# A two-group encoder layer: the opening in a fixed order with the filter network first, and output sums kept in SBUF with products of 512 columns

## The chip, the cores and the metric

The kernel runs on one core of one Trainium2 chip. The metric is the device time of one execution in microseconds (us). All data comes from DRAM and goes back to it within that time. The engines of a core are named as in the profile: PE (TensorE, matrix products), PEld (its weight loads), DVE (VectorE), ACT (ScalarE), POOL (GpSimd) and SP (SyncE, which here issues every DMA).

## What is computed

One encoder layer is applied to two groups of tokens with the same weights: P, the prompt, of 1024 tokens, and S, the sample, of 512. Each token has D = 1024 channels. Everything is fp32.

```
h = rmsnorm(x, norm_g);  z = h @ w_in            # 4096 columns
hy_in, hy_gate, att_qkv, att_gate = split(z)     # 1536, 512, 1536, 512
x0, x1, vv = split(short_conv(hy_in))
f1 = sin(fr1 * (z_pos @ f_w1 + f_b1))            # the filter network, on positions only
f2 = sin(fr2 * (f1 @ f_w2 + f_b2))
kfilt = (f2 @ f_w3) * decay
y_hy  = rmsnorm(x0 * fft_conv(x1 * vv, kfilt), on_hy) * silu(hy_gate)
y_att = rmsnorm(neighbourhood_attention(q, k, v, rpb), on_att) * silu(att_gate)
out = x + concat(y_hy, y_att) @ w_out
```

The attention has 8 heads of 64 channels; tokens stand on a grid 64 wide, and each looks at a window of 8 rows and 16 columns.

## The kernel before, in words

**Numbers.** Every fp32 product is made of three products of rounded halves: a value is split into `hi` (the value rounded to fp32r, a cast) and `lo` (the rest, a subtraction), and hi·hi, lo·hi and hi·lo are summed in PSUM. So a weight unit of 128x512 takes a cast `whi` (L364) and a subtraction `wlo` on POOL (L365).

**Order.** A scheduler of the tile framework puts each engine's instructions into an order, by priorities and a timeline of its own; `high_priority(n)` in the code raises them. Phases are generators that `weave` steps in turn, by fractions that `plan` takes from a list in `run` (L1129). Weight units are loaded and split ahead of use in the order of that plan (`fetch_w`, `issue_w`, `take_w`). All DMAs are issued on SP, one queue, in the order there.

**The opening (0 to 75 us).** `x_norm` (L217) loads four tiles of x (128 tokens x 1024) for each half of P, squares them on ACT with a sum along the row (L229), and DVE makes 1/sqrt of the mean from the sums by shift and three Newton steps (`rsqrt`, L203), then scales the four tiles. `x_turn` (L236) transposes them on PE (L247); ACT writes `hThi` (L249) and DVE `hTlo`. The filter network (`filters_mlp`, L155) runs beside it in segments of 512 positions: a product (L164), then on DVE the argument of the sine reduced to one period (`arg`, `n`), then Sin on ACT (L178). Its last results are `hm_p` and `hm_s`. `w3`, `fc` and `dftm` are constants that are split in the same stretch.

**265 to 885 us** hold the Hyena branch of P, then P's attention beside the Hyena branch and projections of S. The change alters nothing there but `rsqrt`.

**The projections (75 to 265 us)** make q, k, v of P (`proj_tok`, L404, `proj_ch`, L391) beside the spectra of the filters, whose decay tables `dec` come from DRAM.

**The output phase (from 885 us).** Attention of S runs beside the product with w_out, which has two parts: part 0 multiplies the Hyena rows of w_out (y_hy), part 1 the attention rows (y_att). There are three jobs of 512 tokens: P0, P1 and S. A job first loads its four operands `A` (128 channels x 512 tokens), and splits each into `hi` and `lo` (L1073 and a POOL subtraction). Part 0 of P0 and P1 comes first, then their part 1, then part 0 of S, and when the attention is over part 1 of S. For each 256 columns of w_out (two weight units) and each pair of token tiles, 24 products of 128x256 go into one PSUM bank (L1094). P0 and S gather their sums in `acc` in SBUF, which is first loaded with x. P1 does not: ACT copies its part 0 to `oo` (L1106), a DMA stores it to `sum` in DRAM, and in part 1 it is read back as `oy`, x as `ox`, both are added on POOL, and DVE adds the product.

The attention of S ends with `ya`, a 128x512 output block for each pair of heads: DVE multiplies it by the gate `ga_s` (loaded into a tile `qkr`), a DMA stores it as `A_s`, and the output phase loads it again as `lo`.

## Time and profile before

| what | value |
| --- | --- |
| device time, median of 3 runs | 1091.8 us (1089.95 to 1094.8) |
| the profiled execution | 1090.92 us, span of the profile 1089.1 us |
| granted clock of PE, mean | 0.982 |
| busy in the span | PE 92%, PEld 83%, DVE 73%, ACT 43%, POOL 38% |
| chain that ended last | PE 48%, DVE 27%, DMA 12% |

The span is the execution as the profiler saw it on the core. Busy shares are averages over phases with different limits, so what one phase is worth is read in that phase. A row of a timeline gives the start, the duration and, in brackets, how long the engine was idle before and what released it. The granted clock is a share of full speed: 1.00 is 2.4 GHz, 0.50 is 1.2 GHz.

### The profile page before, as it was taken

What the parts mean: (1) busy time and instruction counts of PE and PEld (TensorE: products, weight loads), DVE (VectorE), ACT (ScalarE), POOL (GpSimd) and SP (SyncE); (2) the same over time, 40 slices, a digit from 0 to 9 for tenths busy, and PEclk for the clock granted to TensorE, in tenths of its full rate; (3) what the DMA queues carried; (4) which work ended last, traced back from release to release, by engine and by line L of the source; (5) the groups of instructions that cost most, each with busy time, mean ns of one, the idle gap of its engine ahead of it and who ended that gap; (6) DMA issues with size and microseconds to landing.
All of it is one profiled execution on the core that took longest, in us unless ns stands there. A gap on an engine that the chain in (4) does not pass through costs nothing.

```text
span 1089.1 us, 18072 instructions
## 1 busy us (share of the span) xinstructions
PE 1003.6 (92%) x6444; PEld 906.6 (83%) x6444; DVE 800.1 (73%) x2134; ACT 463.1 (43%) x958; POOL 415.5 (38%) x336
## 2 busy tenths in 40 slices
PE   3898999988999999999989999987989989899997
PEld 2698999977788888888877887876968879899987
DVE  5997779552157767967559999887967977587874
ACT  6453334233331323122124565655747653476530
POOL 2032332112142323123256344354254356784651
PEclk9999999999999999999989999999999999999999
DMA  8226372756312121212483354435544478966522
GB/s 299 69 78 195 119 235 91 242 161 241 109 39 80 58 62 58 67 54 92 173 240 106 94 145 130 129 100 168 141 133 115 132 237 263 295 183 211 173 72 97
DMA packets 112216, 154.84 MB, mean 142 GB/s; under 512 B 7953, under 2 KB 80475, under 8 KB 111615
## 3 DMA queue, kind: packets, MB, share of 16 engines
q1 hardware_dynamic: 112127, 153.69, 45.3%
q8 instruction: 51, 0.84, 0.3%
q14 instruction: 38, 0.31, 0.1%
HBM read 110.35 MB, written 43.32 MB: 141 GB/s over the span
## 4 chain that ended last, share of the span: by engine, by line
PE 48%; DVE 27%; DMA 12%; issue 5%; ACT 4%; SPq 2%; POOL 1%; POOLq 0%; DVEq 0%; ACTq 0%
PE bank L391 25%; PE bank L1094 7%; PE bank L443 3%; PE bank L404 3%; DMA dec<-in_dec_p_dram 2%; PE bank L1012 2%; SPq L60 2%; DVE zc L63 2%; DMA v_p<-vg 2%; DMA v_s<-vg 2%; PE bank L445 2%; PE bank L444 2%; DVE s_sb L981 2%; PE bank L1003 2%; DVE s L63 1%
## 5 line engine op out<-in xcount | busy, mean ns | idle before, releaser
L365 POOL TENSOR_TENSOR wlo<-wraw,whi 128x512 fp32r<-128x512 f32 x160 | 233.7, 1464 | 514.3 <-ACT whi L364 322.5
L391 PE MATMUL bank<-hThi_p,whi 128*128 128x512 f32 x320 | 126.8, 396 | 3.9 <-DVE vg L63 3.2
L391 PE MATMUL bank<-hThi_p,wlo 128*128 128x512 f32 x320 | 126.7, 396 | 0.0
L391 PE MATMUL bank<-hTlo_p,whi 128*128 128x512 f32 x320 | 126.3, 395 | 0.0
L404 PE MATMUL bank<-whi,hThi_p 128*128 128x256 f32 x384 | 111.6, 293 | 6.3 <-DVE vg L63 3.2
L1094 PE MATMUL bank<-whi,hi 128*128 128x256 f32 x384 | 111.6, 292 | 6.0 <-ACT oo L1106 2.6
L1094 PE MATMUL bank<-whi,lo 128*128 128x256 f32 x384 | 110.7, 292 | 0.9 <-POOL lo L63 0.9
L1094 PE MATMUL bank<-wlo,hi 128*128 128x256 f32 x384 | 110.9, 290 | 0.0
L404 PE MATMUL bank<-wlo,hThi_p 128*128 128x256 f32 x384 | 110.6, 289 | 0.0
L404 PE MATMUL bank<-whi,hTlo_p 128*128 128x256 f32 x384 | 108.4, 287 | 0.0
L985 ACT ACTIVATE s_sb<-s_sb,mx 128x360 f32<-128x360 f32 (+1 forms) x96 | 60.3, 629 | 88.2 <-DVE mx L981 87.8
L364 ACT CAST whi<-wraw 128x512 fp32r<-128x512 f32 x66 | 40.9, 623 | 108.0 <-PE bank L391 72.9
L1094 PEld LDWEIGHTS bank<-whi,hi 128*128 128x128 f32 x384 | 75.4, 196 | 7.4 <-ACT oo L1106 2.8
L404 PEld LDWEIGHTS bank<-whi,hThi_p 128*128 128x128 f32 x384 | 74.2, 194 | 8.2 <-DVE vg L63 3.7
L364 DVE CAST whi<-wraw 128x512 fp32r<-128x512 f32 x94 | 58.6, 626 | 27.6 <-POOL lo L63 6.8
L1094 PEld LDWEIGHTS bank<-whi,lo 128*128 128x128 f32 x384 | 74.6, 196 | 1.6 <-POOL lo L63 1.6
L404 PEld LDWEIGHTS bank<-wlo,hThi_p 128*128 128x128 f32 x384 | 74.5, 194 | 1.0 <-issue 1.0
L1094 PEld LDWEIGHTS bank<-wlo,hi 128*128 128x128 f32 x384 | 75.2, 196 | 0.0
L391 PEld LDWEIGHTS bank<-hThi_p,whi 128*128 128x128 f32 x320 | 60.4, 189 | 17.1 <-DVE vg L63 4.1
L404 PEld LDWEIGHTS bank<-whi,hTlo_p 128*128 128x128 f32 x384 | 73.3, 193 | 0.3 <-issue 0.2
L391 PE MATMUL bank<-hThi_s,whi 128*128 128x512 f32 x160 | 65.6, 413 | 8.4 <-DVE vg L63 4.9
L1012 PE MATMUL bank<-pt,V 120*64 120x256 f32 (+1 forms) x352 | 66.5, 295 | 6.6 <-DVE pt L63 4.2
(279 smaller groups left out, 2765.8 us busy)
## 6 DMA issues: line engine op xcount, KB each, us to landing
wraw<-in_w_ch_dram SPq DMA_DIRECT2D x40, 512.0 KB
wraw<-in_w_tk_dram SPq DMA_DIRECT2D x24, 512.0 KB
wraw<-in_w_out_dram SPq DMA_DIRECT2D x16, 512.0 KB
V<-v_p SPq DMA_DIRECT2D x32, 240.0 KB
v_p<-vg SPq DMA_DIRECT2D x32, 160.0 KB
K_p<-Kw SPq DMA_DIRECT2D x4, 1088.0 KB
x<-in_x_prompt_dram SPq DMA_DIRECT2D x8, 512.0 KB
dec<-in_dec_p_dram SPq DMA_DIRECT2D x16, 256.0 KB
```

What stands on the lines that cost most here:

```text
L60: eng.dma_start(out=out, in_=in_)
L63: (eng or self.nc.vector).tensor_tensor(out=out, in0=a, in1=b, op=op)
L364: next(self.w_round)(out=hi, in_=r)
L365: nc.gpsimd.tensor_tensor(out=lo, in0=r, in1=f32(hi), op=ALU.subtract)
L391: nc.tensor.matmul(ps, lhsT=w, rhs=h[s][:, k], start=(k == 0 and i == 0), stop=(k == KC - 1 and i == 2))
L404: nc.tensor.matmul(pss[t // 2][:, t % 2, :], lhsT=h[t // 4][:, k, t % 4 * P:(t % 4 + 1) * P], rhs=w, start=(k == 0 and i == 0 and t % 2 == ...
L443: mm(o, lhsT=c, rhs=z, start=True, stop=False)
L444: mm(o[:, 0:P], lhsT=ns if inverse else s, rhs=z[:, 1], start=False, stop=False)
L445: mm(o[:, P:], lhsT=s if inverse else ns, rhs=z[:, 0], start=False, stop=True)
L985: nc.scalar.activation(out=s_sb[:, :n], in_=s_sb[:, :n], func=AF.Exp, bias=mx, scale=-1.0, accum_out=l)
L1012: nc.tensor.matmul(o, lhsT=vl, rhs=pr_, start=(c == 0 and i == 0), stop=(c == ncu - 1 and i == 1))
L1094: nc.tensor.matmul(ps[:, j, :], lhsT=h[:, tok], rhs=w, start=(k == 0 and i == 0 and j == 0), stop=(k == 3 and i == 2 and j == 1))
```

## The change

It has four parts.

1. In the opening z_p and the filter network's first two weights are loaded ahead of x, and the network's first segment stands ahead of the norm. DVE's order there is the order of the code (`manual_schedule`): first segment, norm and turn of half 0, norm and turn of half 1, and only then the other segments.
2. The sine's argument takes two multiply-adds instead of three, a Newton step of `rsqrt` three instructions instead of four.
3. The first two `wlo` are made by DVE, the others by POOL as before.
4. In the output phase products have 512 columns, every job has its `acc` in SBUF (no `sum`, `oo`, `oy`, `ox`), the Hyena rows of all three jobs are multiplied in one pass over the weights, and eight halves of weights may stand ready from the start. The attention rows of S remain for the end.

```
 rsqrt, in the loop of three:
-            self.mul(t, t, h)
-            self.ts(t, t, -0.5, ALU.mult, 1.5, ALU.add)
-            self.mul(y, y, t)
+            self.stt(t, t, -0.5, h, ALU.mult)
+            self.stt(y, t, 1.5, y, ALU.mult, ALU.add)
 sine argument:
-                self.stt(arg, n, -c1, arg)
-                self.stt(arg, n, -c2, arg)
-                self.stt(arg, n, -c3, arg)
+        self.stt(arg, n, -c1, arg)
+        self.stt(arg, n, c1 - TWO_PI, arg)
 setup, issue_w:
+        self.w_low = itertools.chain([nc.vector] * 2, itertools.repeat(nc.gpsimd))
-            nc.gpsimd.tensor_tensor(out=lo, in0=r, in1=f32(hi), op=ALU.subtract)
+            self.sub(lo, r, f32(hi), next(self.w_low))
 run, the opening:
-        with self.tc.high_priority(4000):
-            self.x_norm(Gp, xp, [lambda: None] * 3 + [self.issue_w] + [lambda: None] * 3 + [self.issue_w])
-            self.x_turn(Gp, (hp0, hp1))
-        self.mlp_load()
-        for _ in zip(self.filters_mlp(Gp, mp), self.filters_mlp(Gs, mp)):
-            pass
+        with self.tc.high_priority(4000), self.tc.manual_schedule(engines={self.nc.vector.engine}):
+            self.mlp_load(Gp)
+            self.mlp_seg(Gp, mp, 0, 0)
+            self.x_norm(Gp, 0, xp)
+            self.issue_w()
+            self.x_turn(Gp, 0, hp0)
+            self.x_norm(Gp, 1, xp)
+            self.issue_w()
+            self.x_turn(Gp, 1, hp1)
+            self.mlp_load(Gs)
+            self.mlp_seg(Gp, mp, 0, 1)
+            self.mlp_seg(Gs, mp, 0, 0)
+        for G, sg in ((Gp, 0), (Gp, 1), (Gs, 0)):
+            self.mlp_seg(G, mp, 1, sg)
 run, the plan and the output phase:
-            [(["out0", "out1", "out0"], (0.0, 0.97), 0), (["att_s"], (0.0, 0.9), 4000)],
-            [(["out1"], every, 0)],
+            [(["out0", "out1"], (0.0, 0.97), 0), (["att_s"], (0.0, 0.9), 4000)],
+            [(["out1s"], every, 0)],
-                dict(G=Gp, seg=1, ops=pools["ops1"], first=pools["first"], last=pools["last"]),
+                dict(G=Gp, seg=1, ops=pools["ops1"], accs=pools["acc1"]),
+        self.w_pools, self.w_bufs = itertools.cycle((wp, self.wp)), 8
-        self.weave(self.chain(self.out_part(0, jobs[:2]), self.then(more_w), self.out_part(1, jobs[:2]), self.out_part(0, jobs[2:])),
-                   self.attention(Gs, ap))
+        self.weave(self.chain(self.out_part(0, jobs), self.out_part(1, jobs[:2])), self.attention(Gs, ap))
 load_w (new), for w_out; other weights are loaded as before:
+        _, h, part, u = key
+        for g in range(2):
+            self.dma(raw.rearrange("p (k g c) -> p k g c", k=2, g=2)[:, :, g],
+                     self.io["w_out"][h * 2 + g, part].rearrange("p (k c) -> p k c", k=4)[:, u * 2:u * 2 + 2])
 out_part, behind the loads of the operands, as it is now:
+        for h in range(2):
+            hs = slice(h * 512, (h + 1) * 512)
+            units = [self.take_w(("w_out", h, part, k // 2)) for k in range(4)]
             for jb in jobs:
+                G, t0, acc = jb["G"], jb["seg"] * 4, jb["acc"]
                 r = G.ratt if part else G.rhy
+                if part == 0:
+                    self.dma(acc[:, :, hs], G.x[t0 * P:(t0 + 4) * P, hs].rearrange("(t p) c -> p t c", p=P))
+                for t in range(4):
+                    ps = self.bank(next(self.mm_tags))
+                    tok = slice(t * P, (t + 1) * P)
+                    for k, (whi, wlo) in enumerate(units):
+                        hi, lo = jb["hi"][k][:, tok], jb["lo"][k][:, tok]
+                        for i, (w, a) in enumerate(((whi, hi), (wlo, hi), (whi, lo))):
+                            nc.tensor.matmul(ps, lhsT=a, rhs=w, start=(k == 0 and i == 0), stop=(k == 3 and i == 2))
+                    o = acc[:, t, hs]
+                    self.stt(o, ps, r[:, t0 + t:t0 + t + 1], o)
                     if part == 1:
+                        self.dma(G.out[(t0 + t) * P:(t0 + t + 1) * P, hs], o)
+                yield
```

`mlp_seg` is one segment of `filters_mlp`, `x_norm` and `x_turn` are now called once for each half.

What moves is the order on the engines. First DVE in the opening, from the first scaling of x on. Before (`rs_...` are steps of the second half's `rsqrt`, `w3lof`, `w3lob`, `fc` and `dftm` splits of constants, `arg` and `n` the filter network):

```order
L79 TENSOR_SCALAR x<-x,rs_y_201 128x1024 x4
L75 SCALAR_TENSOR_TENSOR hTlo_p<-bank,pc,hThi_p 128x512 x3
L81 TENSOR_SCALAR rs_h_249<-ss 128x4
L79 TENSOR_SCALAR rs_y_250<-rs_h_249 128x4
L81 TENSOR_SCALAR rs_y_250<-rs_y_250 128x4
L63 TENSOR_TENSOR w3lof<-w_477,w3f 64x512 x2
L63 TENSOR_TENSOR rs_t_251<-rs_y_250 128x4
L81 TENSOR_SCALAR arg<-bank,pc 128x512
L63 TENSOR_TENSOR fc<-fc 128x512
L63 TENSOR_TENSOR w3lob<-w_477,w3b 64x512 x2
```

There the second scaling follows after 39 more rows, with network steps all between them. The same stretch now:

```order
L80 TENSOR_SCALAR x<-x,rs_y_207 128x1024 x4
L64 TENSOR_TENSOR wlo<-wraw,whi 128x512 x2
L76 SCALAR_TENSOR_TENSOR hTlo_p<-bank,pc,hThi_p 128x512 x3
L64 TENSOR_TENSOR fc<-fc 128x512
L64 TENSOR_TENSOR w3lof<-w_467,w3f 64x512 x2
L64 TENSOR_TENSOR dftm<-km_481 128x256
L64 TENSOR_TENSOR dftm<-km_485 128x256
L64 TENSOR_TENSOR w3lob<-w_467,w3b 64x512 x2
L76 SCALAR_TENSOR_TENSOR hTlo_p<-bank,pc,hThi_p 128x512 x3
```

No `arg` or `n` stands there any more; five more `dftm`, two more `hTlo` and the second `rsqrt` lead to the second scaling, behind which eight `hTlo` stand together ahead of the next `arg`:

```order
L64 TENSOR_TENSOR rs_t_312<-rs_y_311 128x4
L76 SCALAR_TENSOR_TENSOR rs_t_312<-rs_t_312,rs_h_310 128x4
L76 SCALAR_TENSOR_TENSOR rs_y_311<-rs_t_312,rs_y_311 128x4
L80 TENSOR_SCALAR x<-x,rs_y_311 128x1024 x4
L76 SCALAR_TENSOR_TENSOR hTlo_p<-bank,pc,hThi_p 128x512 x8
L82 TENSOR_SCALAR arg<-bank,pc 128x512
```

The second place is SP at the end of the program. Before, the last four reloads of A_s (`lo_...`) stood together, behind the attention's last loads:

```order
L60 DMA qkr<-in_rpb_dram 128x1x488
L60 DMA A_s_108<-ya 128x512
L60 DMA V<-v_s_124 120x3x128
L60 DMA V<-v_s_125 120x3x128
L60 DMA lo_12096<-A_s_106 128x512
L60 DMA lo_12097<-A_s_107 128x512
L60 DMA lo_12098<-A_s_108 128x512
L60 DMA qkr<-ga_s_113 128x512
L60 DMA A_s_109<-ya 128x512
L60 DMA lo_12099<-A_s_109 128x512
L60 DMA out_dram<-acc 128x2x256 x8
```

Now each stands near the store that it reads, with loads of the attention behind it (the numbers of the tiles are others, `A_s_107` and `A_s_108` are the last two blocks):

```order
L61 DMA qkr<-in_rpb_dram 128x1x488
L61 DMA A_s_107<-ya 128x512
L61 DMA out_dram<-acc 128x512
L61 DMA lo_11432<-A_s_107 128x512
L61 DMA out_dram<-acc 128x512
L61 DMA V<-v_s_123 120x3x128
L61 DMA out_dram<-acc 128x512
L61 DMA V<-v_s_124 120x3x128
L61 DMA qkr<-ga_s_112 128x512
L61 DMA A_s_108<-ya 128x512
L61 DMA lo_11433<-A_s_108 128x512
L61 DMA out_dram<-acc 128x512 x8
```

The gate `ga_s` of the last block no longer has three reloads ahead of it. On PE the output products stand, by count, before the first transposes of the sample's attention (L929) 187 before and 84 now, from there to its last value product (L1012) 758 and 423, behind that 207 and 69; one of the products now is as wide as two before.

## Rows read from the trace of the kernel before

**Rows 1.** The page, busy time and share of the span of each engine.

```profile
PE 1003.6 (92%) x6444; PEld 906.6 (83%) x6444; DVE 800.1 (73%) x2134; ACT 463.1 (43%) x958; POOL 415.5 (38%) x336
```

**Rows 2.** Windows by phase: length, busy PE, PEld, DVE, ACT, POOL, clock, DMA share, GB/s.

```profile
0.00:75.00 75.00, 51.67 (x365) 45.64 (x366) 61.59 (x135) 44.00 (x77) 11.85 (x16) 0.98 0.43 155
75.00:265.00 190.00, 177.00 (x1313) 168.52 (x1311) 126.78 (x394) 66.01 (x164) 49.61 (x38) 0.99 0.53 176
...
885.00:1089.00 204.00, 186.76 (x1478) 183.02 (x1478) 145.15 (x353) 88.64 (x199) 121.63 (x110) 0.97 0.63 196
```

**Rows 3.** Timeline of DVE: start, us, line, operation, out<-in, shapes, count, idle before.

```profile
10.08 0.17 DVE L81 TENSOR_SCALAR rs_h<-ss 128x4 f32<-128x4 f32 x1 [10.08 <-ACT xsq L229]
...
10.89 1.22 DVE L63 TENSOR_TENSOR rs_t<-rs_t,rs_h 128x4 f32<-128x4 f32 x1
...
17.20 2.74 DVE L79 TENSOR_SCALAR x<-x,rs_y 128x1024 f32<-128x1024 f32 x4
21.24 2.07 DVE L75 SCALAR_TENSOR_TENSOR hTlo_p<-bank,pc,hThi_p 128x512 fp32r<-128x512 f32 x3 [1.29 <-ACT hThi_p L249]
...
23.93 1.38 DVE L63 TENSOR_TENSOR w3lof<-w,w3f 64x512 fp32r<-64x512 f32 x2
...
44.19 2.74 DVE L79 TENSOR_SCALAR x<-x,rs_y 128x1024 f32<-128x1024 f32 x4
...
73.89 0.69 DVE L63 TENSOR_TENSOR hm_s<-arg,hm_s 64x512 fp32r<-64x512 f32 x1
...
1060.07 1.75 DVE L75 SCALAR_TENSOR_TENSOR ya<-ya,pc,qkr 128x512 f32<-128x512 f32 x1 [1.18 <-DMA qkr<-ga_s]
```

**Rows 4.** Timeline of PE, opening and output phase.

```profile
42.67 2.07 PE L164 MATMUL bank<-h_p,w 128*128 128x512 f32 x2 [4.21 <-DVE arg L81]
...
939.06 0.39 PE L1094 MATMUL bank<-whi,hi 128*128 128x256 f32 x1 [2.63 <-ACT oo L1106]
...
1054.18 0.75 PE L1012 MATMUL bank<-pt,V 120*64 120x256 f32 x5
...
1070.52 0.28 PE L1094 MATMUL bank<-wlo,hi 128*128 128x256 f32 x1
...
1084.67 0.28 PE L1094 MATMUL bank<-whi,lo 128*128 128x256 f32 x1
```

**Rows 5.** The chain that ended last: start, us, what.

```profile
87.64 7.25 DMA dec<-in_dec_p_dram
...
280.71 33.17 PE bank L391 x145
...
925.99 12.07 DMA sum<-oo
...
1061.85 1.99 DMA A_s<-ya
1063.90 2.59 DMA lo<-A_s
...
1068.60 1.68 PE bank L1094 x12
```

**Rows 6.** Timeline of SP's queue, opening and end: start, us of issue, what.

```profile
1.19 1.84 SPq L60 DMA_DIRECT2D x<-in_x_prompt_dram  x4
...
7.55 1.63 SPq L60 DMA_DIRECT2D w<-in_w_dram  x2
10.11 0.31 SPq L60 DMA_DIRECT2D z_p<-in_z_p_dram  x1
...
1054.02 2.34 SPq L60 DMA_DIRECT2D lo<-A_s  x3
```

**Rows 7.** Timeline of ACT, the table load and the first two Sin.

```profile
39.85 1.28 ACT L178 ACT_TABLE_LOAD   x1
41.15 1.15 ACT L178 ACTIVATE h_p<-arg 128x512 f32<-128x512 f32 x2
```

**Rows 8.** Timeline of POOL in the opening.

```profile
10.82 4.94 POOL L365 TENSOR_TENSOR wlo<-wraw,whi 128x512 fp32r<-128x512 f32 x4 [9.51 <-ACT whi L364]
```

More of the change, by code (lines that the diff above doesn't have):

```diff
@@ L156, in filters_mlp, with mlp_seg @@
+    def mlp_seg(self, G, mp, layer, s):
         nc = self.nc
[L157 to L182 removed]
@@ new lines, in mlp_seg @@
+        w, b, fr = self.w12[layer], self.v[f"b{layer + 1}"], self.v[f"fr{layer + 1}"]
+        sl = slice(s * 512, (s + 1) * 512)
+        if not layer and not s:
+            self.h1[G.name] = mp.tile([P, G.L], F32, name=f"h1_{G.name}")
+        h = self.h1[G.name] if layer else self.z[G.name]
+        ps = self.bank("ml")
+        nc.tensor.matmul(ps, lhsT=w, rhs=h[:, sl], start=True, stop=True)
+        arg = mp.tile([P, 512], F32, name="arg", bufs=2)
+        self.ts(arg, ps, b, ALU.add, fr, ALU.mult)
@@ new lines, in mlp_seg @@
+        n = mp.tile([P, 512], F32, name="n", bufs=2)
+        magic = 12582912.0
+        self.ts(n, arg, 1.0 / TWO_PI, ALU.mult, magic, ALU.add)
+        self.ts(n, n, magic, ALU.subtract)
+        c1 = 6.28125
+        self.stt(arg, n, -c1, arg)
+        self.stt(arg, n, c1 - TWO_PI, arg)
+        self.ts(arg, arg, 3.1415925, ALU.min, -3.1415925, ALU.max)
+        nc.scalar.activation(out=arg if layer else self.h1[G.name][:, sl], in_=arg, func=AF.Sin)
+        if layer:
+            self.stack([t[:, sl] for t in self.hm[G.name]], arg)
@@ L211, in rsqrt, with x_norm @@
             self.mul(t, y, y)
[L212 to L214 removed]
+            self.stt(t, t, -0.5, h, ALU.mult)
+            self.stt(y, t, 1.5, y, ALU.mult, ALU.add)
         return y
[L218 removed]
+    def x_norm(self, G, s, xp):
         nc = self.nc
[L221 to L236 removed]
@@ L238, in x_turn @@
[L238 to L250 removed]
+        ss = xp.tile([P, 4], F32, name="ss", bufs=2)
@@ new lines, in x_norm @@
+        xs = []
+        for j in range(4):
+            tt = s * 4 + j
+            x = xp.tile([P, D], F32, name="x", bufs=G.nt)
+            self.dma(x, G.x[tt * P:(tt + 1) * P, :])
+            sq = xp.tile([P, D], F32, name="xsq", bufs=1)
+            nc.scalar.activation(out=sq, in_=x, func=AF.Square, accum_out=ss[:, j:j + 1])
+            xs.append(x)
+        if not s:
+            self.fetch_w()
+        r = self.rsqrt(xp, ss, 4, 1.0 / D, "x")
+        for j in range(4):
+            self.ts(xs[j], xs[j], r[:, j:j + 1])
@@ new lines, in x_norm, with x_turn @@
+        G.xs += xs
+    def x_turn(self, G, s, hp):
+        nc = self.nc
+        hi = hp.tile([P, KC, 512], F32R, name=f"hThi_{G.name}")
+        lo = hp.tile([P, KC, 512], F32R, name=f"hTlo_{G.name}")
+        G.hi.append(hi)
+        G.lo.append(lo)
+        for k in range(KC):
+            ps = self.bank()
+            for j in range(4):
+                nc.tensor.transpose(out=ps[:, j * P:(j + 1) * P], in_=G.xs[s * 4 + j][:, k * P:(k + 1) * P], identity=self.ident)
+            gk = self.v["norm_g"][:, k:k + 1]
+            nc.scalar.activation(out=hi[:, k], in_=ps, func=AF.Copy, scale=gk)
+            self.stt(lo[:, k], ps, gk, f32(hi[:, k]), ALU.subtract)
@@ L310, in steps @@
         if what[:3] == "out":
-            return [[]] + [[("w_out", g, int(what[3]))] for g in range(4)]
+            n = {"out0": 3, "out1": 2, "out1s": 1}[what]
+            return [[]] + [[("w_out", h, int(what[3]), u) for u in range(2)] if j == 0 else [] for h in range(2) for j in range(n)]
         return [[] for _ in range({"k": 20, "att_p": 33, "att_s": 17}[what])]
@@ L1074, in out_part @@
                 self.sub(lo, a, f32(hi), nc.gpsimd)
-            if part == 0 and "accs" in jb:
+            if part == 0:
                 jb["acc"] = jb["accs"].tile([P, 4, D], F32, name="acc")
         yield
-        for g in range(4):
-            gs = slice(g * 256, (g + 1) * 256)
-            units = [[t.rearrange("p (k c) -> p k c", c=256) for t in self.take_w(("w_out", g, part))] for _ in range(2)]
+        for h in range(2):
+            hs = slice(h * 512, (h + 1) * 512)
+            units = [self.take_w(("w_out", h, part, k // 2)) for k in range(4)]
@@ L1117, in out_part @@
                     if part == 1:
-                        self.dma(rows(G.out), o)
-            yield
+                        self.dma(G.out[(t0 + t) * P:(t0 + t + 1) * P, hs], o)
+                yield
     @staticmethod
@@ L1219, in run @@
         cms, pools = [], {}
-        for n in ("ops0", "ops1", "acc0", "first", "last", "ops2", "acc2"):
+        for n in ("ops0", "ops1", "acc0", "acc1", "ops2", "acc2"):
             c, pools[n] = opn(n, "right")
```

106 lines of the change are left out of this document (13 added, 93 removed).

## The prediction

> **What bounds the kernel now.** I read the page's engine table first: TensorE (PE) is busy for 1003.6 of 1089.1 us [rows 1]. A share over the whole span tells nothing of where a change pays, so the second view is the windows by phase [rows 2]: in the opening (0 to 75 us) PE is busy for 51.7 of 75 us, in the projections (75 to 265) 177.0 of 190, in the output phase (885 to 1089) 186.8 of 204. Between those, 265 to 885, the change touches only a three-instruction saving in each rsqrt. So 23 us of PE idleness in the opening, 13 in the projections and 17 in the output phase is all that better order can win; shorter products come on top.
>
> The third view is the timeline of the opening. PE can start nothing before VectorE (DVE) has scaled the four x tiles, at 17.20 us, and the second half's tiles are scaled only at 44.19 [rows 3]: their rsqrt began about 23 us and was spread out between steps of the filter MLP. PE meanwhile runs dry: at 42.67 it had waited 4.21 us, for an MLP product that itself hung on DVE [rows 4]. The fourth view is the output phase: PE stands 2.63 us for the copies `oo`, which wait for a store of the sums to DRAM that took 12.07 us [rows 4, 5]. At the end a chain of single steps runs from the last attention product at 1054.18 over `ya`, its store and its reload, until the remaining products can follow [rows 3 to 5].
>
> **Part 1, the opening.** *Later start.* On SP, two loads of w (1.63 us of issue) and z_p (0.31) now go ahead of x, which starts at 1.19 before [rows 6]: x moves by 1.94 us. On ScalarE the table load (1.28) and one Sin (1.15 for two, so 0.58) stand ahead of the fourth square [rows 7]. The sums of squares were there at 10.08 [rows 3], so now at 10.08 + 1.94 + 1.86 = 13.9. Then the rsqrt: it took 10.08 to 17.20, 7.1 us for 15 instructions, since four of them took about 1.2 us instead of 0.17 beside the four subtractions `wlo` on POOL (10.82 to 15.76) [rows 3, 8]. Now it has 12 instructions, at 0.2 us a step 2.4 us; two of the four subtractions have gone to DVE, behind the scaling, and the two that stay may each hold up one or two steps; I take 2 us for them. First scaling: 13.9 + 4.4 = 18.3, **1.1 us later** than before.
>
> The Trainium skill, "SBUF — State Buffer", section "Who interferes with whom", says that DVE with two inputs in SBUF, or in a two-port mode, and a GpSimd instruction block each other for the whole instruction. The four long steps agree with it. By that rule each subtraction left on POOL could hold DVE for a whole instruction, 2.5 us in all where I take 2.
>
> *Second half sooner.* The first `hTlo` stood 4.04 us behind the scaling (21.24 - 17.20) [rows 3]; the two subtractions now on DVE, two of 0.7 us by the nearest row (`w3lof` [rows 3]), fall into the 1.29 us that it waited there. So it starts at 22.4. From there to the second scaling the new order has eight `hTlo` (0.69 each, 5.5), `w3` (four of 0.69, 2.8), `fc` (as one of those, 0.7), seven `dftm` (256 columns each, half of a `w3` step's 512, so 0.35 each, 2.4) and an rsqrt (2.4): 13.8 us. Second scaling: 36.2, **8.0 us sooner** than 44.19. Behind it stand only the eight `hTlo`, no MLP instruction.
>
> *The MLP.* DVE is busy for 61.6 of the 75 us, all of it from 17 on. Removed from that stretch are six steps of the sine's argument (0.6 to 0.69 each, about 4) and the first segment's six instructions (about 3), which now run while x is still loading; added are 1.1 of later start and 1.4 of subtractions. The last `hm` at 73.89 [rows 3] moves by about **-4 us**.
>
> *What that is worth.* PE gains 8 us of lead, the filters 4. The projections that follow use PE for 177 of 190 us, and in the chain their start is held by transfers, a decay load of 7.25 us at 87.64 among them [rows 2, 5], which come no sooner. I take the middle, **-6 us**. Bounds: -8 (all of PE's lead stays) and +1.1 (only the later start is seen). On SP the order behind x is the same.
>
> **Part 2, rsqrt elsewhere.** Three steps of 0.2 us in each of some 16 others is 9.6 us of DVE time, nearly all hidden behind PE; **-0.5 us**, bounds 0 and -2.
>
> **Part 3, the output phase.** *Products.* 118 steps of 128x256 take 14.15 us (1070.52 to 1084.67), 0.1199 each; 145 of 128x512 take 33.17, 0.2288 each [rows 4, 5]. One wide product replaces two: 576 x (0.2398 - 0.2288) = 6.3 us.
>
> The Trainium skill, "TensorE: Matmul & The Clock Gate", section "Back-to-back issue gap", speaks against this: it gives the isolated spacing as columns / 2.4 GHz plus 2.5 ns, so a pair saves 2.5 ns and the 576 save 1.4 us. The rows show 11 ns a pair.
>
> *Along the path.* The sample's attention sets the pace, so I count by the products on PE ahead of, between and behind its steps, in the issue order of the two kernels. Ahead of its first transposes: 187 x 0.1199 = 22.4 before, 84 x 0.2288 = 19.2 now, -3.2. Between them and the last value product: 758 (90.9) before, 423 (96.8) now, +5.9. The wait of 2.63 for `oo` goes with the DRAM round trip: -2.6; sixteen `oo`, eight adds on POOL, eight writes of sums and sixteen reloads (`oy`, `ox`) go too, all beside PE: nothing more. The first output column now needs four weight halves instead of two, each with a `wlo` of some 1.24 us on POOL (4.94 for four [rows 8]): between 0 and 2.5, I take half, +1.3. Their loads are 24 of 256 KB in 1 KB runs instead of 16 of 512 KB; they are asked for ahead of use, eight halves deep from the start, so I cost them at nothing; if they came late, the next half of the output columns would be late, on PE directly. The tail: before, the last value product (1054.93) to the last output product (1084.95) took 30.0 us. The products that need the last reload could go on at 1068.60, 13.7 us after the attention's end; `ga_s`, for which DVE waited at 1060.07, stood on SP behind three reloads of A_s (2.34 us of issue) [rows 3, 6], which now go out earlier. So 11.4; nine of the 69 products left fit inside, and 60 x 0.2288 = 13.7 follow: 25.1, -4.9. Sum: -3.2 + 5.9 - 2.6 + 1.3 - 4.9 = **-3.5 us**. Bounds: -8.9 (6.3 of products and 2.6 of wait, nothing lost) and +2.4 (-3.2 + 5.9 + 2.5 - 2.8: the wait gone into another one, 2.5 for the halves, no product inside the tail's gap).
>
> Evictions of 128x512 onto `acc` replace twice as many of 128x256; DVE is busy for 145 of 204 us here [rows 2], so that is hidden. If it came late, a PSUM bank would be late next.
>
> **Sum.** -6 - 0.5 - 3.5 = -10.0 against the profiled execution's 1090.9: 1080.9. The median of the runs is 0.9 higher: **1082 us**. Its own range from these parts is 1077 to 1086.
>
> **Rivals.**
> A, both gains whole. PE keeps the 8 us, since it was the one short of work, and the output phase gives 8.9: 1091.8 - 17.4 = 1074. For it speaks PE's 92% [rows 1]; against it the decay loads [rows 5] and the attention's pace.
> B, the opening is swallowed. The filters' first transfers hold them as before, whenever the MLP ends, and the projections wait behind the filters; then only the output phase shows: 1088. For it speaks the 7.25 us load in the chain [rows 5]; against it that SP issues loads as buffers come free, and these would come free sooner.
> C, slower. In the new order on SP two of the three earlier reloads `lo` from A_s stand one or two transfers behind the store that they read, in the middle of the phase, and no longer at its end. SP is one queue: it holds until that store has landed, and the attention's next loads (V, bias rows, q and k) wait behind it. A store in this phase took 12.07 us to land [rows 5]. If both holds take that long and pass wholly into the attention, 24.1 against -10.0: 1106. It decides from about 8 us a hold on (16 against the 10.0 and the 5.5 that make it a loss that can be told). Against it: loads are issued ahead of use, and at the tail a store and its reload had landed 4.64 us after the store's issue (1061.85 to 1066.49) [rows 5].
> D, a wide product costs nearly two narrow ones here: 0.2373 instead of 0.2288 on 567 of them on the path, +4.8: 1087. Against it stands the row of 512 columns [rows 5]; for it, that none of them stands in this phase. It is what the Trainium skill's section above comes to.
>
> **Chances.** Forecast 0.46, A 0.19, B 0.20, D 0.03, C 0.12. A measurement of this kernel can tell about 0.5% (5.5 us) from no change. Faster by more: the forecast, A and a part of D, 0.66. Within it: B and the rest of D, 0.22. Slower: C, 0.12. The range of 8 in 10 takes in A's and B's sizes with 2 or 3 us of spread, and leaves out C and the edges: 1071 to 1093.
>
> **What would show it.** Right: the first scaling at 18 to 19 us, the second at 35 to 38, no PE gap of 4 us near 40; the last `hm` near 70; 128x512 output products spaced at 0.229; no wait for `oo`; the last reload's product about 11 us behind the last value product. Wrong: SP waiting for A_s stores with attention behind it (C); the phase borders at 265 unmoved although the opening is shorter (B); output products spaced at 0.237 (D); or a second half that is scaled as late as before.

## The result and the profile after

The changed kernel took 1079.24 us (median; 1074.62 to 1081.36), against 1092.12 for the kernel before (1089.95 to 1094.8) beside it: a ratio of 0.9874 (95% interval 0.9836 to 0.9912). Against the 1091.8 shown above that is 12.6 us less; 10 were forecast. The sum was near, but its terms were not: most of the gain came from a place that the prediction costs at nothing, the order of SP's queue between 265 and 885 us.

The profiled execution of the changed kernel took 1074.62 us, the fastest of its runs and 4.6 below their median. So a single phase's length below may be some us off from run to run; what separates the parts is the medians of the experiments.

The page, busy time of each engine (compare [rows 1]):

```profile
PE 996.7 (93%) x5868; PEld 877.5 (82%) x5868; DVE 788.4 (73%) x2036; ACT 455.0 (42%) x942; POOL 394.9 (37%) x318
```

576 products and 98 DVE instructions fewer, and PE is busy for 6.9 us less: about the 6.3 that wide products were to save. Windows by phase, with the columns of [rows 2], first the two of before that did not stand there, then after:

```profile
265.00:550.00 285.00, 281.43 (x1393) 238.44 (x1394) 182.89 (x531) 73.04 (x128) 85.99 (x48) 0.99 0.27 88
550.00:885.00 335.00, 306.77 (x1901) 270.99 (x1900) 283.73 (x724) 191.38 (x391) 146.40 (x127) 0.97 0.47 134
```

```profile
0.00:75.00 75.00, 55.14 (x383) 47.82 (x384) 54.91 (x122) 40.44 (x72) 10.94 (x14) 0.98 0.43 148
75.00:265.00 190.00, 171.62 (x1260) 164.09 (x1259) 129.34 (x367) 65.44 (x157) 45.82 (x35) 0.96 0.51 165
265.00:550.00 285.00, 285.00 (x1426) 242.60 (x1425) 184.41 (x537) 76.28 (x141) 90.95 (x50) 1.00 0.29 96
550.00:885.00 335.00, 313.45 (x1950) 279.80 (x1949) 291.71 (x723) 195.69 (x400) 160.14 (x136) 0.97 0.51 149
```

In the opening PE is busy for 3.5 us more, in the projections for 5.4 less, from 265 to 550 for 3.6 more: by 550 us PE has been busy for 511.8 us against 510.1. The large step is 550 to 885, where the change only shortens `rsqrt`: PE is busy for 6.7 us more.

Windows of fixed times mix early and late work, so I set marks by what SP issues: the last store of P's attention (`A_p<-cx`), the first and last store of the sample's v (`v_s<-vg`), the last store of its gate (`ga_s<-vg`). Each time is the start of that row in SP's timeline; the output phase runs from the last mark to the end of the span.

| us | before | after | difference |
| --- | --- | --- | --- |
| last A_p | 545.2 | 545.8 | +0.6 |
| to the first v_s | 200.5 | 197.5 | -3.0 |
| to the last v_s | 61.4 | 51.9 | -9.5 |
| to the last ga_s | 74.5 | 73.2 | -1.3 |
| output phase | 207.5 | 204.5 | -3.0 |

The 61.4 us in which v of S is made became 51.9. SP's timeline in that stretch, the two places where ACT was late before:

```profile
745.72 1.41 SPq L60 DMA_DIRECT2D v_s<-vg  x3
747.22 0.57 SPq L60 DMA_DIRECT2D qkr<-in_rpb_dram  x1
747.84 0.53 SPq L60 DMA_DIRECT2D v_s<-vg  x1
...
786.92 1.41 SPq L60 DMA_DIRECT2D v_s<-vg  x3
788.42 0.57 SPq L60 DMA_DIRECT2D qkr<-in_rpb_dram  x1
789.09 0.46 SPq L60 DMA_DIRECT2D wraw<-in_w_ch_dram  x1
789.61 1.00 SPq L60 DMA_DIRECT2D v_s<-vg  x1
```

After, the first of them:

```profile
743.27 2.27 SPq L61 DMA_DIRECT2D v_s<-vg  x4
745.64 0.39 SPq L61 DMA_DIRECT2D wraw<-in_w_ch_dram  x1
746.32 0.58 SPq L61 DMA_DIRECT2D qkr<-in_rpb_dram  x1
```

Four stores empty one tile `vg`, of which there is one buffer. Before, the load of a bias row, and the second time a weight unit too, stood ahead of the fourth store; now the four go first. What waits is ACT's next cast into `vg`, then DVE's subtraction into the same tile, and behind that PE, whose bank these two read. The waits of ACT from 740 to 812 us (engine, tile and line, what it waited for: total us, times, longest), before and after:

```profile
ACT vg L845 <- DMA v_s<-vg: 13.8, 2, 7.9
```

```profile
ACT vg L852 <- DMA v_s<-vg: 6.0, 2, 3.3
```

The waits of PE for `vg` in the same window, before and after:

```profile
PE bank L391 <- DVE vg L63: 4.9, 1, 4.9
PE bank L404 <- DVE vg L63: 2.3, 1, 2.3
```

```profile
PE bank L398 <- DVE vg L64: 0.5, 1, 0.5
```

From the first to the last `v_s` PE was busy for 52.3 of 61.4 us before, and for 51.3 of 51.9 after.

In the chain of before the two fourth stores are among its longest pieces:

```profile
747.84 8.16 DMA v_s<-vg
...
789.61 9.24 DMA v_s<-vg
```

### The profile page after: what moved, and what is told of

It reads as the page before. It is cut to its first block, busy times and chain, and to the rows that moved or that the text cites. A ratio compares the mean times of both kernels' runs of the same rounds, so it can differ in the third digit from the quotient of the medians.

```text
span 1072.8 us, 16738 instructions
## 1 busy us (share of the span) xinstructions
PE 996.7 (93%) x5868; PEld 877.5 (82%) x5868; DVE 788.4 (73%) x2036; ACT 455.0 (42%) x942; POOL 394.9 (37%) x318
## 4 chain that ended last, share of the span: by engine, by line
PE 59%; DVE 20%; DMA 11%; ACT 4%; issue 3%; SPq 1%; POOL 1%; DVEq 0%; ACTq 0%; POOLq 0%
PE bank L398 28%; PE bank L1098 9%; PE bank L411 4%; PE bank L450 4%; DMA dec<-in_dec_p_dram 3%; PE bank L1019 2%; PE bank L452 2%; PE bank L451 2%; PE bank L1010 2%; DVE zc L64 1%; DVE s_sb L988 1%; SPq L61 1%; DVE whi L371 1%; DMA K_s<-Kw 1%; DVE xk L64 1%
## 5 line engine op out<-in xcount | busy, mean ns | idle before, releaser
L64 POOL TENSOR_TENSOR wlo<-wraw,whi 128x512 fp32r<-128x512 f32 x150 | 222.0, 1486 | 483.9 <-ACT whi L371 341.3
L1098 PE MATMUL bank<-whi,hi 128*128 128x512 f32 x192 | 78.4, 410 | 6.4 <-ACT hi L1079 4.6
L1098 PE MATMUL bank<-wlo,hi 128*128 128x512 f32 x192 | 77.3, 403 | 0.0
L1098 PE MATMUL bank<-whi,lo 128*128 128x512 f32 x192 | 76.8, 404 | 0.0
L398 PEld LDWEIGHTS bank<-hThi_p,wlo 128*128 128x128 f32 x320 | 60.6, 189 | 12.1
L398 PEld LDWEIGHTS bank<-hTlo_p,whi 128*128 128x128 f32 x320 | 60.4, 189 | 12.0
L64 POOL TENSOR_TENSOR T<-cmask,qkr 128x480 f32<-128x480 f32 x32 | 39.5, 1242 | 67.4 <-DMA qkr<-in_rpb_dram 49.2
L64 DVE TENSOR_TENSOR pt<-bank,pt 120x384 fp32r<-120x384 f32 (+1 forms) x96 | 56.1, 595 | 11.0 <-ACT pt L1012 10.3
```

Source lines behind the costliest of these rows:

```text
L64: (eng or self.nc.vector).tensor_tensor(out=out, in0=a, in1=b, op=op)
L398: nc.tensor.matmul(ps, lhsT=w, rhs=h[s][:, k], start=(k == 0 and i == 0), stop=(k == KC - 1 and i == 2))
L1098: nc.tensor.matmul(ps, lhsT=a, rhs=w, start=(k == 0 and i == 0), stop=(k == 3 and i == 2))
```

## Experiments

**The theories.** One: the gain lies in that order of SP, and it was the shorter `rsqrt` and sine (part 2) that tipped the scheduler into it. The rivals: the opening (parts 1 and 3) brought it, or the output phase (part 4) did, as forecast. Every kernel was compared with the kernel before on the same chip. The experiments ran on several chips, on which the kernel before has medians of 1092.1 to 1095.5 us; so two of them are compared by these ratios and their intervals, and a few us between their medians say little.

### The store order alone

`v_first` is the kernel before with one priority:

```
+                        with ExitStack() as st:
+                            if G.name == "s":
+                                st.enter_context(self.tc.high_priority(6000))
-                        self.dma(dst[rr, :, m * 2:(m + 1) * 2, :], ...)
+                            self.dma(dst[rr, :, m * 2:(m + 1) * 2, :], ...)
```

> Edit: the kernel before, with nothing changed but the priority of the sample's eight v stores per weight half group (v_s<-vg), so that on SP the fourth store of a tile stands ahead of the bias-row load (qkr<-in_rpb) and the w_ch load instead of behind them, as it does in the changed kernel. Theory T1 (most of the gain is this order on SP, brought about by the scheduler and not by any of the four parts): 9 to 13 us faster than before, about 1081, and the last w_in product of the sample (880.5 in the trace before, 867.2 after) near 868 to 870. Rival T2 (the shorter rsqrt and sine themselves save it on DVE): no change, 1092, and 880. Rival T3 (the profiled execution before had a chance stall): no change against the before of the same rounds.

Measured: 0.989 (0.9849 to 0.9931), 1080.04 us. The order of every engine is that of before up to the first of these stores. SP's timeline now has the four together, ahead of the loads, and ACT's wait is short:

```profile
784.27 2.12 SPq L60 DMA_DIRECT2D v_s<-vg  x4
786.49 0.85 SPq L60 DMA_DIRECT2D wraw<-in_w_ch_dram  x1
787.44 0.58 SPq L60 DMA_DIRECT2D qkr<-in_rpb_dram  x1
```

```profile
ACT vg L845 <- DMA v_s<-vg: 4.5, 2, 3.2
```

So a priority on these stores gives 12 us, with nothing of the change in the kernel. Not all of it lies between the first and the last of the stores: that stretch is 6.9 us shorter than before (the table of marks below), with PE busy for 53.4 of its 54.5 us. Behind the first stores the scheduler also put other instructions into another order, on PE from 791 us on, so what the order of the stores is worth with all else in the old order was not isolated. The last product of the sample's projections started at 871.2, a little later than the 868 to 870 expected.

### Each part alone, and each left out

Parts as numbered above under "The change"; 1 and 3 go together, since both concern the opening.

`short_only`, part 2 in the kernel before:

```
-            self.mul(t, t, h)
-            self.ts(t, t, -0.5, ALU.mult, 1.5, ALU.add)
-            self.mul(y, y, t)
+            self.stt(t, t, -0.5, h, ALU.mult)
+            self.stt(y, t, 1.5, y, ALU.mult, ALU.add)
...
-                self.stt(arg, n, -c2, arg)
-                self.stt(arg, n, -c3, arg)
+                self.stt(arg, n, c1 - TWO_PI, arg)
```

> Edit: the kernel before with part 2 alone (two multiply-adds in the sine's argument, three instructions in a Newton step). In the issue order the four v stores of a tile stand together here, as in the changed kernel. T1 (order on SP): 9 to 13 us faster, about 1081, last w_in product near 868 to 870. T2 (DVE time saved): the same time, so it does not tell T1 and T2 apart alone, only with v_first. My prediction's own account (0.5 us for part 2): 1091.5.

Measured: 0.9917 (0.9886 to 0.9947), 1083.61 us.

`out_only`, part 4 in the kernel before:

```
-            [(["out0", "out1", "out0"], (0.0, 0.97), 0), (["att_s"], (0.0, 0.9), 4000)],
+            [(["out0", "out1"], (0.0, 0.97), 0), (["att_s"], (0.0, 0.9), 4000)],
...
+                            nc.tensor.matmul(ps, lhsT=a, rhs=w, start=(k == 0 and i == 0), stop=(k == 3 and i == 2))
```

> Edit: the kernel before with part 4 alone (128x512 products, all sums in SBUF, hyena rows in one pass). In the issue order the bias-row load still stands ahead of the fourth v store. T1: only the output phase's gain, -3 to -4 us, about 1088; last w_in product at 880. If the output phase were the main gain: -10 or more, 1082 or less.

Measured: 1.0047 (1.0023 to 1.007), 1097.19 us. A gain of 3 to 4 us was expected; it is slower.

`open_only`, parts 1 and 3 in the kernel before:

```
-        with self.tc.high_priority(4000):
+        with self.tc.high_priority(4000), self.tc.manual_schedule(engines={self.nc.vector.engine}):
+            self.mlp_load(Gp)
+            self.mlp_seg(Gp, mp, 0, 0)
...
-            nc.gpsimd.tensor_tensor(out=lo, in0=r, in1=f32(hi), op=ALU.subtract)
+            self.sub(lo, r, f32(hi), next(self.w_low))
```

> Edit: the kernel before with parts 1 and 3 alone (opening in a fixed order on DVE, first two wlo on DVE; sine and rsqrt as before). The bias-row load stands ahead of the fourth v store. T1 with a swallowed opening: within 2 us of before, 1091 to 1094; the last store of the Hyena rows of P (A_p<-cx, 545.2 before, 545.8 after) near 546. My prediction's account of the opening: -6, 1086.

Measured: 0.9997 (0.997 to 1.0023), 1090.63 us.

`no_short`, the changed kernel without part 2:

```
-            self.stt(t, t, -0.5, h, ALU.mult)
-            self.stt(y, t, 1.5, y, ALU.mult, ALU.add)
+            self.mul(t, t, h)
+            self.ts(t, t, -0.5, ALU.mult, 1.5, ALU.add)
+            self.mul(y, y, t)
...
-        self.stt(arg, n, c1 - TWO_PI, arg)
+        c2 = 0.0019350051879882812
+        self.stt(arg, n, -c2, arg)
+        self.stt(arg, n, c1 + c2 - TWO_PI, arg)
```

> Edit: the changed kernel without part 2 (three multiply-adds and four Newton instructions as before). In its issue order the bias-row load stands ahead of the fourth v store again. T1 (the store order on SP makes the gain): 10 to 14 us slower than the changed kernel, 1090 to 1095, with the stretch from the first to the last v_s store at 61 to 62 us as before (51.9 in the changed kernel). If parts 1 and 4 carried the gain, as predicted: about 1080.

Measured: 1.0025 (1.0008 to 1.0043), 1096.38 us, somewhat more than the 1090 to 1095 expected. The whole gain is gone, and its chain has the two long stores again:

```profile
749.96 8.51 DMA v_s<-vg
...
791.92 9.27 DMA v_s<-vg
```

`no_open`, the changed kernel without parts 1 and 3:

```
-        with self.tc.high_priority(4000), self.tc.manual_schedule(engines={self.nc.vector.engine}):
+        with self.tc.high_priority(4000):
...
-            self.sub(lo, r, f32(hi), next(self.w_low))
+            nc.gpsimd.tensor_tensor(out=lo, in0=r, in1=f32(hi), op=ALU.subtract)
```

> Edit: the changed kernel without parts 1 and 3 (opening as before; short sine and rsqrt, output phase as changed). The v stores stand together. If the opening is worth nothing, as its own run showed (0.9997 [0.997, 1.0023]): 1078 to 1081, the same as the changed kernel. If its 8 us of PE lead arrive at the end in company with the other parts: 1085 or more.

Measured: 0.9895 (0.9868 to 0.9922), 1081.06 us.

`no_out`, the changed kernel without part 4:

```
-        for h in range(2):
-            hs = slice(h * 512, (h + 1) * 512)
+        for g in range(4):
+            gs = slice(g * 256, (g + 1) * 256)
```

> Edit: the changed kernel without part 4 (opening and short arithmetic as changed, output phase as before). The v stores stand together. If part 4 is worth 3 to 4 us with the new order: 1082 to 1084, like part 2 alone (1083.6). If part 4 costs time, as it did alone (1.0047): 1075 or less.

Measured: 0.9883 (0.9862 to 0.9903), 1080.21 us, below the 1082 to 1084 expected if part 4 gained beside the new order and above the 1075 expected if it cost time there.

From the differences of these ratios, times 1092 us, each part's worth beside the others (each uncertain by some 3 to 5 us):

| part | in the kernel before | beside one other part | beside all others |
| --- | --- | --- | --- |
| 1 and 3, opening | -0.3 | -3.7 (with 2), -2.4 (with 4) | -2.3 |
| 2, short steps | -9.1 | -12.4 (with 1, 3), -16.6 (with 4) | -16.5 |
| 4, output phase | +5.1 | -2.4 (with 2), +3.1 (with 1, 3) | -1.0 |

The marks of each profiled execution, read as above, show where:

| kernel | last A_p at | A_p to last ga_s | of it first to last v_s | output phase |
| --- | --- | --- | --- | --- |
| before | 545.2 | 336.4 | 61.4 | 207.5 |
| open_only | 546.8 | 335.7 | 62.0 | 204.9 |
| out_only | 548.9 | 336.6 | 61.2 | 212.3 |
| no_short | 547.8 | 336.2 | 61.4 | 210.6 |
| v_first | 548.6 | 324.0 | 54.5 | 205.2 |
| short_only | 551.5 | 321.7 | 50.9 | 208.9 |
| no_open | 548.5 | 322.6 | 50.3 | 209.3 |
| no_out | 545.2 | 321.6 | 49.9 | 211.6 |
| after | 545.8 | 322.5 | 51.9 | 204.5 |

The third column falls in two groups, 335.7 to 336.6 and 321.6 to 324.0. The long one stands in all four kernels with the old `rsqrt` and sine and no priority on the stores; `v_first` has the old steps and the short value. So the order of SP suffices for what part 2 gives, without the shorter steps. No kernel has the shorter steps with the old order of SP, so their own time was not separated; `short_only` gives no more than `v_first` (0.9917 against 0.989). Some 3 of the 14 us between the groups stand ahead of the first `v_s`, and `v_first` has them too (197.4 us there against 200.5), though every engine's order is that of before up to that store: those 3 do not come from the order of the stores, and from what was not found. Why shorter DVE steps make the scheduler put those stores first was not tried.

### The width of the products

`narrow` is the changed kernel with each output product cut in two of 256 columns:

```
-                        for i, (w, a) in enumerate(((whi, hi), (wlo, hi), (whi, lo))):
-                            nc.tensor.matmul(ps, lhsT=a, rhs=w, start=(k == 0 and i == 0), stop=(k == 3 and i == 2))
+                        for c in range(2):
+                            cs = slice(c * 256, (c + 1) * 256)
+                            for i, (w, a) in enumerate(((whi, hi), (wlo, hi), (whi, lo))):
+                                nc.tensor.matmul(ps[:, cs], lhsT=a, rhs=w[:, cs], start=(k == 0 and i == 0 and c == 0), stop=(k == 3 and i == 2 and c == 1))
```

> Edit: the changed kernel with each product of the output phase split into two of 128x256 (1152 instead of 576), all else as changed; the scheduler puts them elsewhere among the attention. If the width is worth what the rows say (11 ns a pair on 576 pairs): 4 to 6.5 us slower than the changed kernel, 1083 to 1086. If the output phase is set by the attention's chain and the products only fill: within 2 us of it. If finer products are worth more to the order than their width costs: faster.

Measured: 0.9813 (0.9789 to 0.9837), 1073.92 us: not slower by the 6 us that the products cost more, but 5.3 us below the median of the changed kernel (the two intervals just touch). The price of a product was as forecast (after, in the chain: 60 of 512 columns in 13.91 us, 0.232 each). The cut changes the width and, with it, the scheduler's order; so the run shows that the width did not pay on balance, not what it costs on the path. Why `narrow` is faster was not isolated: its profiled execution took 1075.76 us, that of the changed kernel 1074.62. In the order of PE 244 narrow products are left behind the last value product, where 69 wide ones were, so more work covers the attention's last steps, and PE does not stop there.

### The reload of A_s

`direct` is the changed kernel with the last three attention blocks of S kept in SBUF, where the change stores and reloads them:

```
+            if pr and G.direct:
+                self.stt(G.direct[pr - 1], y, v["on_att"][:, pr:pr + 1], ga, ALU.mult)
+                return
...
-                self.dma(a, self.A_d[G.name][part * 4 + k][:, sl])
+                if part and k and G.direct:
+                    a = G.direct[k - 1]
+                else:
+                    self.dma(a, self.A_d[G.name][part * 4 + k][:, sl])
```

> Edit: the changed kernel, but the last three attention blocks of the sample are left in SBUF (6 KB a partition) instead of being stored as A_s and loaded again as lo; the order on PE stays the same but for a few rows. Theory (SP's holds of rival C do cost, though less than the gain elsewhere, and the tail's chain runs over the store and the reload): SP waited 6.9 us in three for the A_s stores, and the last store and reload took 1.99 and 2.55 us: 6 to 10 us faster than the changed kernel, 1069 to 1073; the tail from the last gated block to the end 22 to 23 us instead of 27. Rival (holds are hidden, only the tail counts): 4 to 5 us, 1075. Rival (something else is late next in the tail, the rsqrt of the attention's sums or POOL): under 2 us.

Measured: 0.9818 (0.9782 to 0.9853), 1073.68 us, 5.6 below the changed kernel's median (the two intervals just overlap), between the 6 to 10 us expected if the holds cost time and the 4 to 5 if only the tail does. The holds that rival C spoke of are real. SP's timeline of the changed kernel near the end:

```profile
1020.58 0.42 SPq L61 DMA_DIRECT2D A_s<-ya  x1
1021.74 0.34 SPq L61 DMA_DIRECT2D out_dram<-acc  x1
1026.52 0.32 SPq L61 DMA_DIRECT2D lo<-A_s  x1
1028.62 0.34 SPq L61 DMA_DIRECT2D out_dram<-acc  x1
1029.06 0.39 SPq L61 DMA_DIRECT2D V<-v_s  x1
```

SP stands from 1022.08 to 1026.52 for the store's landing, and V of the attention goes out behind it. The waits of SP from 860 us on, before and in the changed kernel:

```profile
SPq L60 <- DMA A_s<-ya: 1.7, 1, 1.7
```

```profile
SPq L61 <- DMA A_s<-ya: 6.9, 3, 4.4
```

In `direct` there is no such row. Over the kernels with part 4 the total of these holds and the output phase go up together: `direct` 0 and 201.7 us, after 6.9 and 204.5, `no_open` 8.3 and 209.3, `no_short` 10.6 and 210.6, `out_only` 10.8 and 212.3 (`narrow`, 8.5 and 207.2, lies between). That is one profile of each, so a trend, not a price, and the kernels with the old output phase, with 1.7 us of such holds or none, differ as much (204.9 to 211.6).

What the profile of `direct` shows as gained lies in the tail: from the end of the last value product to the end of the last output product it takes 22.7 us, the changed kernel 26.8, since the last store and reload are gone. From the last ga_s to that value product, where the holds stand, it is not shorter (174.9 us against 174.0). So the holds are shown, but not that they cost time; where the rest of the 5.6 us lies is not known.

### DVE's fixed order in the opening

`free_dve` lets the scheduler order DVE again:

```
-        with self.tc.high_priority(4000), self.tc.manual_schedule(engines={self.nc.vector.engine}):
+        with self.tc.high_priority(4000):
```

> Edit: the changed kernel without the fixed order of DVE in the opening; the calls stay in their new order, and the scheduler places the filter network's steps between the others again. Theory (the fixed order makes the filters late: their first decay load goes out at 86.9 instead of 70.9 to 78, and DVE waits some 7 us idle between 39 and 53): the filters come 5 to 10 us sooner, the second half's scaling some 5 us later, and the time is within 3 us of the changed kernel, since the opening's changes hardly reach 545 us. If PE's lead were what counts: 3 to 8 us slower.

Measured: 0.9908 (0.9875 to 0.9942), 1083.98 us, 4.7 above the changed kernel's median where 3 were expected at most; the two intervals overlap. Its marks are those of the changed kernel until the last ga_s (546.8 and 322.2); only the output phase is longer, 214.6 us, with 12.3 us of holds for A_s:

```profile
SPq L61 <- DMA A_s<-ya: 12.3, 3, 6.2
```

So the fixed order brought nothing where it stands, though much moved there: without it the second half is scaled at 43.78 us and the last `hm` starts at 65.73 (39.82 and 86.10 in the changed kernel). An edit 900 us ahead changed the order of the output phase.

### Together, and the wait for vg taken away

`direct_narrow` has both edits above:

```
+            if pr and G.direct:
...
+                        for c in range(2):
```

> Edit: both the split into products of 128x256 and the last three blocks left in SBUF. If the two gains add: 1064 to 1068 (narrow gave 0.9813 against the changed kernel's 0.9874 of before). If they take the same wait away, finer products filling the tail's gap and the holds: 1070 to 1074, no better than narrow.

Measured: 0.9757 (0.9719 to 0.9794), 1067.56 us, the best of all, below `narrow` and `direct`, and inside the 1064 to 1068 expected if the two gains add. Its output phase takes 199.1 us. PE does not stop at the attention's end. The windows of its last stretch, columns as in [rows 2]:

```profile
1038.00:1048.00 10.00, 10.00 (x86) 10.00 (x85) 9.33 (x22) 0.62 (x1) 6.84 (x5) 1.00 0.15 54
1048.00:1058.00 10.00, 10.00 (x86) 10.00 (x85) 3.49 (x5) 0.00 (x0) 0.00 (x0) 1.00 0.36 133
```

The same stretch of the changed kernel:

```profile
1038.00:1048.00 10.00, 5.00 (x26) 3.94 (x26) 5.63 (x13) 2.31 (x5) 1.26 (x1) 0.80 0.07 26
1048.00:1058.00 10.00, 6.63 (x21) 5.06 (x22) 3.63 (x13) 0.62 (x1) 1.27 (x1) 0.69 0.31 103
```

`direct_narrow_vg2` has in addition two buffers of `vg` for S:

```
-                vh = tp.tile([P, 2, 4, P], F32R, name="vg", bufs=1)
+                vh = tp.tile([P, 2, 4, P], F32R, name="vg", bufs=2 if G.name == "s" else 1)
...
-        gap.tile([P, 1920], F32, name="gap")
+        gap.tile([P, 896], F32, name="gap")
```

> Edit: as the run before (products of 128x256, last three attention blocks left in SBUF), and the tile vg from which the sample's v is stored has two buffers instead of one, so that the cast of the next tile no longer waits for the landing of the four stores. If that wait, 6.0 us in two in the changed kernel and 13.8 in the kernel before, passes into the time: 3 to 6 us faster than 1067.6, 1062 to 1065, with no wait of ACT for v_s left. Rival (PE is fed from elsewhere in the meantime, and only the long waits of the old order reach it): within 2 us of 1067.6.

Measured: 0.979 (0.9758 to 0.9823), 1072.32 us: 3 to 6 us less than `direct_narrow` were expected if the wait passes into the time, and it is not faster (the two intervals overlap). ACT no longer waits for `v_s`, but v of S takes no less: the last two stores start 50.8 us after the first, in `direct_narrow` 50.0, and the last ga_s goes out at 869.0, there at 868.9. In `direct_narrow` PE was already busy for 49.7 of those 50.0 us. So the waits of some 3 us that the good order leaves are hidden; of the two of before, 13.8 us in all, a part reached PE (7.2 us of waits, above). The output phase of this profile, 204.8 against 199.1, is 5.7 us longer; why was not tried.

## Why the prediction was right, and where it was not

**The sum** was right by the time and wrong by its parts. Added one after the other in ratios, part 2 gives -9.1, the opening -3.7 and part 4 -1.0: -13.8 in all, where -0.5, -6 and -3.5 were forecast. In another sequence the shares are others (the table above): the opening alone gives nothing, part 4 alone costs time. That the total lies within 3 us of the 1082 forecast is luck: a gain that was not foreseen made up for two that were smaller than forecast. Rival A, both of those whole, is out with them.

**Part 2** is the term that failed most. "Nearly all hidden behind PE" was not tested by itself; nothing speaks against it for the 9.6 us of DVE time. The step that failed is the sentence that the change touches only a three-instruction saving between 265 and 885 us (the description of the kernel says so too): the order of another engine, SP, changed there as well. I had compared the two orders in the opening and in the output phase, not between.

**The opening.** DVE's timeline after (columns as in [rows 3]):

```profile
16.76 1.12 DVE L64 TENSOR_TENSOR rs_t<-rs_y 128x4 f32<-128x4 f32 x1
17.92 1.19 DVE L76 SCALAR_TENSOR_TENSOR rs_t<-rs_t,rs_h 128x4 f32<-128x4 f32 x1
...
19.34 2.74 DVE L80 TENSOR_SCALAR x<-x,rs_y 128x1024 f32<-128x1024 f32 x4
...
35.72 0.42 DVE L64 TENSOR_TENSOR dftm<-km 128x256 f32<-128x256 f32 x1 [1.10 <-DMA km<-in_kmat_dram]
...
39.82 2.74 DVE L80 TENSOR_SCALAR x<-x,rs_y 128x1024 f32<-128x1024 f32 x4
...
52.34 0.75 DVE L76 SCALAR_TENSOR_TENSOR hTlo_p<-bank,pc,hThi_p 128x512 fp32r<-128x512 f32 x1 [1.11 <-ACT hThi_p L245]
...
85.38 1.41 DVE L64 TENSOR_TENSOR hm_s<-arg,hm_s 64x512 fp32r<-64x512 f32 x2 [0.15 <-ACT hm_s L185]
```

The first scaling came at 19.34 (forecast 18.3); the `rsqrt` took the 4.4 us forecast, its sums came at 14.97 instead of 13.9. Two `rsqrt` steps were long, 1.12 and 1.19 us, where 2 us were taken for them. They run beside the two `wlo` left on POOL. The Trainium skill, "SBUF — State Buffer", section "Who interferes with whom", says that a DVE instruction with two inputs in SBUF and a GpSimd instruction that reads SBUF get in each other's way; the trace agrees with it. The second scaling came at 39.82 instead of 44.19, not at 36.2: `dftm` waited for its loads `km` (2.1 us in three waits), and all began 1.0 later.

The step that failed first is the MLP: not 4 us sooner, but 12.2 us later (the last `hm`, the second of the row at 85.38, starts at 86.10 instead of 73.89). I had taken away from DVE's busy time and held it to stay busy. In its fixed order it does not: from 17 to 53 us it is busy for 27.9 of 36 us (33.5 before), and all later segments stand behind eight `hTlo` that wait for ACT. From 53 on it is busy for 32.8 of 34 us, but with steps of the projections (`qss`, `px`, their `rsqrt`) between those of the segments. The first decay load went out at 86.87 instead of 70.87, the last spectrum of S was stored at 280.9 instead of 251.9. "On SP the order behind x is the same" does not hold either: a store of k and a weight load now stand ahead of that decay load.

The other step that failed is the worth of PE's lead. By 75 us PE had been busy for 3.5 us more, not 8, and the projections took 5.4 back, so by 265 us nothing was left. In the time that is rival B's result, but B's reason is not shown: `free_dve` has its filters some 20 us sooner than the changed kernel and reaches the last A_p no sooner (546.8 against 545.8). What takes the lead back stays open. The opening is worth 0 to -3.7 us (each uncertain by 3 to 5), inside the bounds of -8 and +1.1, in three of the four comparisons nearer to B's 0 than to -6.

**The output phase.** The products' price was right (0.232 against 0.2288), D is out as to the price. The wait for `oo` went. The tail had three terms. Last value product to the reload's product: 1042.3 to 1051.00, 8.7 us, better than the 11.4 forecast. But nothing of the 69 products filled it; all followed it, the first nine slowly (1051.00 to 1055.19). PE's timeline and the chain:

```profile
1045.22 1.87 PE L811 MATMUL bank<-ones,sqs 128*128 128x1 f32 x8 [2.92 <-POOL sqs L64]
1051.00 0.79 PE L1098 MATMUL bank<-whi,hi 128*128 128x512 f32 x1 [3.91 <-ACT hi L1079]
```

```profile
1045.74 1.99 DMA A_s<-ya
1047.75 2.55 DMA lo<-A_s
...
1051.00 3.36 PE bank L1098 x7
...
1055.19 13.91 PE bank L1098 x60
```

So the tail took 26.8 us (to 1069.10) instead of 25.1, which is -3.2 of the -4.9. All profiles with the wide products and the reload have such a tail (26.6 to 27.1 us; 29.5 to 32.0 with the old output phase), so some 3 us of this term are there each time. What failed is the sum for the stretch ahead of it, from the last ga_s to the last value product, about +1.4 by the terms (-3.2 + 5.9 - 2.6 + 1.3). One profile of each shows +8.2 us for part 4 in the kernel before (181.5 against 173.3), +9.5 beside parts 1 and 3, +3.8 beside part 2, and -1.4 beside all (174.0 against 175.4). So alone, in the old order of SP, part 4 turns the sign: +5.1 us, C's side. C's mechanism exists, with 4.4 us at most for one store of the changed kernel where C needed 8, and the prediction has no term for it below that. But `direct`, without the holds, was not shorter in this stretch, so that the holds took the gain is not shown; what did stays open.

**The width.** I priced 576 x 11 ns = 6.3 us into the path. PE's busy time fell by 6.9 us, but `narrow`, without the saving, is no slower; the order that the scheduler made for it must have outweighed the price, which was not isolated. The Trainium skill, "TensorE: Matmul & The Clock Gate", section "Back-to-back issue gap", gives columns / 2.4 GHz plus 2.5 ns as the isolated spacing, by which a pair would save an estimated 2.5 ns. The trace disagrees: two narrow ones at 0.1199 us against one wide at 0.2288 differ by 11 ns.

## What to carry to other kernels

Where a scheduler orders the queues, compare the order of every engine over the whole program, and set marks by phase in the trace, before a gain is credited to the edit; then make the suspected order by one priority and see whether it gives the gain alone (and remember that the scheduler goes on from there with another order). On a queue that serves everything, stores that empty a single-buffered tile go ahead of loads. A reload right behind its own store holds the queue, and at the end of the program it lengthens the tail (26.8 us against 22.7 without it): keep such a block in SBUF. Leave enough independent products behind the last dependent chain, so that PE has something to do while that chain ends.

## What the runs showed of the hardware that was not expected

- The same store `v_s` released ACT's cast 8.16 and 9.24 us after its issue with a bias row, the second time a weight unit too, ahead of it on SP, and 4.35 and 3.59 us after (744.74 to 749.09 and 781.93 to 785.52) with the loads behind it. How much of that each load takes was not measured.
- The granted clock fell to 0.80 and 0.69 in the two windows of the changed kernel where PE stood for 2.92 and 3.91 us, and the products behind the reload came 0.43 us apart at first (3.36 us for seven), near the 1.2 GHz level, then 0.23. In `direct_narrow`, where PE never stopped there, it stayed at 1.00.
